# Triangular inverse of the RWKV-7 chunks: all four quadrants of the array, with the second head's chunk halves exchanged and its transpose made by a product with the identity

## The chip, the cores and the metric

The kernel runs on one core of a Trainium2 chip. The metric is the device time of one execution in microseconds (us). The engines meant below are TensorE (PE, and PEld for its weight loads), VectorE (DVE), ScalarE (ACT), GpSimd (POOL) and SyncE (SP), whose queue issues most of the DMAs.

## The reference, cut to what matters

A decoder trunk of two layers over 512 tokens of width 1024. Each layer is a SwiGLU half step, a mixing stage, and a second SwiGLU half step. The mixing stage projects the tokens once and gives the columns to three branches: attention, RWKV-7 time mixing with 4 heads of 64, and a short convolution. The change touches the RWKV-7 branch alone. Its reference is a scan over tokens:

```python
def step(S, inp):
    r_t, w_t, k_t, v_t, kk_t, a_t = inp
    s_kk = jnp.einsum('bhvk,bhk->bhv', S, kk_t)
    S = (S * w_t[:, :, None, :] - s_kk[..., None] * (kk_t * a_t)[:, :, None, :]
         + v_t[..., None] * k_t[:, :, None, :])
    return S, jnp.einsum('bhvk,bhk->bhv', S, r_t)
```

Because each step also subtracts a rank-one term that depends on the state, a chunked form needs the inverse of a unit triangular matrix for each chunk and head.

## The kernel before

The 512 tokens are 8 chunks of 64. The 4 heads are two pairs, `rwkv(0)` and `rwkv(1)`; each is a Python generator. In a pair, `e` is the head (0 or 1), `b` a block of two chunks, `c` the chunk within its block, and `rows[0]`, `rows[1]` are partitions 0 to 63 and 64 to 127. So each pair works on 16 small matrices of 64 by 64 (2 heads, 4 blocks, 2 chunks), held in tiles of 128 partitions: partitions `rows[c]` hold chunk `c`, and `e`, `b` are in the free direction.

A pair's steps, with the names that are used below:

- `pairs` makes `B_` and `K_` (line 824, PE to `ps_c`; line 828, DVE). `LT` is the triangular part of `B_`.
- `LT` goes to DRAM as `dl` (line 836, SP), and its 16 by 16 diagonal blocks come back as `G` (line 846, eight DMAs). DVE inverts the blocks by elimination: 30 short instructions on `elim` and `inv` (lines 853 and 854). The result goes out as `di` (line 856) and comes back as `C_` (line 859, eight DMAs).
- `px` (`ps_xv`, line 893) is `K_` times the centred values `vN`; `alphas` (`ps_ta`, lines 867 and 878) transposes a part of `AR`. Both are copied by ACT into the tile `AX`. `beN` and `kaN` are two more transposes.
- `T_` (line 907) is the block diagonal inverse and `TT` (line 908) its transpose, made by DVE. Two levels then widen it: `ps_x` is `LT` times `T_`, masked to `X` (line 921); at level 0 `ps_t` corrects `T_` (line 925); at both levels `ps_tt` corrects `TT` (line 928).
- `ps_w` (`ps_w2` in the code, line 935) applies `TT` to `AX`, and ACT negates it back into `AX` (line 936), which is `Wn` from there.
- `ps_gn` gives `GT` and `N` (lines 953 and 954, DVE); `ps_o` (lines 964 to 969) gives `RT` and `y` (lines 971 and 972); then `ps_s` and `St` (lines 977 and 978) carry the state from chunk to chunk, six times; `ps_ys` adds the state's part to `y`; a group norm follows (`ps_v`, `gnrs`) and the gate (`ps_g`).

Products made by the helper `each`, by line 893 and by line 935 read `rows[c]` and write `rows[c]`: two of the array's four 64 by 64 quadrants. `ps_c`, `ps_gn` and `ps_o` read and write both halves in all four combinations.

What sets the order. The big projections of the stage (`ps_mm`, from the generator `products`) are interleaved with the three branches by a credit: each `yield` of a branch states a cost, and product steps are put in between in proportion, from the totals `RWKV_WORK`, `ATT_WORK` and `FILL_WORK` at the top. A scheduler then orders each engine's instructions; within `manual_schedule` PE's rows keep the order written. `behind` adds a wait so that neighbours on the array start together. Each engine runs its queue in order. Accumulators of a pair have the tag `r0` or `r1`, two buffers each, so that a new one waits until an older one has been read.

Of the kernel before, what the change touches and what calls it, by code (L numbers as in the profile page):

```python
# [32 lines left out]
GROUPS = ((0, 12), (12, 22))  # L33
RWKV_WORK, ATT_WORK, FILL_WORK = 29.8, 15.2, 129.6

# [22 lines left out]
def trunk_kernel(ctx, tc, ins, out, layers=L, phases=("ffn1", "mix", "ffn2")):  # L58
# [21 lines left out]
    def psum(shape, name, tag="x"):  # L80
        return ps.tile(shape, F32, name=name, tag=tag, bufs=2)
# [503 lines left out]
    def mix(l, hn, ss, mp, then, ready):  # L585
# [170 lines left out]
        def rwkv(q):  # L756
# [78 lines left out]
            dl = dram.tile([P, 2 * NB, CH], F32, name="dl", tag=f"dl{q}", bufs=2)  # L835
            nc.sync.dma_start(dl, LT.rearrange("p e b t -> p (e b) t"))
            NM = CH // BASE
# [36 lines left out]

            def alphas():
                pt = tmajor(AR[:, 0].rearrange("p c t -> p (c t)"), "ps_ta")
                for e in range(2):
                    nc.scalar.copy(AX[:, e, :, 0], pt[:, :, rows[e]])

# [5 lines left out]
            vN = S(q, "vN")  # L885
            stt(vN.rearrange("p (b d) -> p b d", d=CH), mv.unsqueeze(2).to_broadcast([P, 2 * NB, CH]), -1.0 / CH, pt, ALU.mult, ALU.add)
            vN = blocks(vN)
            yield 0.4
            px = psum([P, 2, NB, CH], "ps_xv", R)
            for e in range(2):  # L890
                for b in range(NB):
                    for c in range(2):
# [14 lines left out]
            tt(T4, C_.unsqueeze(2).to_broadcast([P, 2 * NB, NM, BASE]), msk, ALU.mult)  # L907
# [3 lines left out]
            def each(name, lhs, rhs):  # L911
                pt = psum([P, 2, NB, CH], name, R)
                for e in range(2):
                    for b in range(NB):
                        for c in range(2):
                            mm(pt[rows[c], e, b], lhs[rows[c], e, b], rhs[rows[c], e, b], start=True, stop=True)
                return pt

            for lev in range(2):
                px = each("ps_x", LT, T_)  # L920
                tt(X, px, rep2(f"lev{lev}", NB), ALU.mult)
                yield 1.3
                if lev == 0:
                    p1 = each("ps_t", TT, X)
                    tt(T_, T_, p1, ALU.subtract)
                    yield 1.3
                p2 = each("ps_tt", X, TT)
                tt(TT, TT, p2, ALU.subtract)
                yield 1.3
            Wn = AX.rearrange("p e b a t -> p e b (a t)")  # L930
            for e in range(2):
                pt = psum([P, NB, P], "ps_w2", R)
                for b in range(NB):
                    for c in range(2):
                        mm(pt[rows[c], b], TT[rows[c], e, b], Wn[rows[c], e, b], start=True, stop=True)
                other = nc.scalar.mul(Wn[:, e], pt, -1.0)
                yield 1.1

# [4 lines left out]
            with tc.manual_schedule(engines={mybir.EngineType.PE}):  # L943
                for b in range(NB):
                    for c, e in ce:
                        m = mm(pgs[c][rows[e], 0, b], Wn[rows[c], e, b, :CH], beN[rows[c], b, rows[e]], start=True, stop=True)
                        behind(m, other)
                    for c, e in ce:
                        mm(pgs[c][rows[e], 1, b], kaN[rows[c], b, rows[e]], vN[rows[c], b, rows[e]], start=True, stop=False)
                    for c, e in ce:  # L950
                        mm(pgs[c][rows[e], 1, b], beN[rows[c], b, rows[e]], Wn[rows[c], e, b, CH:], start=False, stop=True)
            for c, pg in enumerate(pgs):
# [8 lines left out]
            with tc.manual_schedule(engines={mybir.EngineType.PE}):  # L961
                for b in range(NB):
                    for c, e in ce:
                        m = mm(pos[c][rows[e], 0, b], Wn[rows[c], e, b, :CH], B_[rows[c], e, b, 1], start=True, stop=True)
                        behind(m, other)
                    for c, e in ce:
                        mm(pos[c][rows[e], 1, b], Wn[rows[c], e, b, CH:], B_[rows[c], e, b, 1], start=True, stop=False)
                    for c, e in ce:
                        mm(pos[c][rows[e], 1, b], vN[rows[c], b, rows[e]], K_[rows[c], e, b, 1], start=False, stop=True)
# [402 lines left out]
```

## Time and profile before

| what | value |
|---|---|
| median of 3 runs | 1913.05 us (1911.36 to 1914.67) |
| the profiled execution | 1913.21 us, of which its span is 1911.2 us |
| PE busy | 1878.8 us, 98% of the span |
| DVE busy | 1399.8 us, 73% |
| ACT busy | 837.0 us, 44% |
| POOL busy | 130.7 us, 7% |

In the profile a line is a line of the kernel, an arrow `a<-b` means that `a` is written from `b`, a tile's number is left out, and the release of an idle engine stands in brackets. A 64 by 64 product in fp32 is two records on PE and PEld, so 16 products of a group are 32 records; a transpose of 128 by 128 is one record, and so is a product of the projections. `ps_w2` appears as `ps_w`.

### The profile page before, as it was taken

The page shows a single profiled execution, that of the slowest core. Times are in us where ns is not written, and L with a number is a line of the kernel's source. Part 1 is how long each engine was busy: PE and PEld are TensorE (multiplying, and loading weights), DVE is VectorE, ACT ScalarE, POOL GpSimd, SP SyncE. Part 2 cuts the span into 40 slices and gives each one's busy share as a digit, 9 for nine tenths or more (in the row PEclk, how much of TensorE's full clock was granted, in tenths as well). Part 3 has the DMA queues.
Part 4 walks back from the last instruction along what each step waited for, and adds up shares of the span by engine and source line. Part 5 has one row for each costly group of instructions (what it writes and reads, how often), then busy time and mean ns, then how long its engine had stood idle before and what let it go on. Part 6 is the DMA issues. An engine that isn't in the chain of part 4 may idle for free. (4 is left out here: it accounts for less than half of the span.)

```text
span 1911.2 us, 37042 instructions
## 1 busy us (share of the span) xinstructions
PE 1878.8 (98%) x15504; PEld 1741.7 (91%) x15504; DVE 1399.8 (73%) x2181; ACT 837.0 (44%) x1264; POOL 130.7 (7%) x212
## 2 busy tenths in 40 slices
PE   8999999999999999999999999999999999999999
PEld 7998899897888999899899989989878899988998
DVE  7687687758976877677877776876599667864862
ACT  4443255346322554155345514544562235532551
POOL 0101100100000001110100020010000000110000
PEclk8999999999999999999999999999999999999999
DMA  7767877521312476887727678781321315774741
GB/s 300 245 168 221 271 198 229 168 70 45 79 43 81 123 198 176 278 218 199 264 62 193 171 260 242 191 278 42 93 61 49 88 34 163 209 217 130 198 140 59
DMA packets 104326, 308.46 MB, mean 161 GB/s; under 512 B 23392, under 2 KB 24416, under 8 KB 103136
## 3 DMA queue, kind: packets, MB, share of 16 engines
q1 hardware_dynamic: 75936, 203.33, 32.9%
q0 software_dynamic: 28224, 102.77, 21.7%
q8 instruction: 121, 1.98, 0.4%
q14 instruction: 45, 0.37, 0.1%
HBM read 302.66 MB, written 3.41 MB: 160 GB/s over the span
## 5 line engine op out<-in xcount | busy, mean ns | idle before, releaser
L101 ACT CAST wH<-wraw 128x1024 fp32r<-128x1024 f32 (+2 forms) x292 | 268.4, 922 | 512.6 <-PE ps_mm L91 176.8
L102 DVE TENSOR_TENSOR wL<-wraw,wH 128x1024 fp32r<-128x1024 f32 (+2 forms) x292 | 308.1, 1058 | 96.9 <-ACT wH L101 95.8
L90 PE MATMUL ps_mm<-actH,wH 128*128 128x512 f32 (+1 forms) x784 | 288.5, 368 | 0.0
L91 PE MATMUL ps_mm<-actL,wH 128*128 128x512 f32 (+1 forms) x784 | 288.0, 367 | 0.0
L92 PE MATMUL ps_mm<-actH,wL 128*128 128x512 f32 (+1 forms) x784 | 288.0, 367 | 0.0
L441 PE MATMUL ps_d<-comH,wH 128*128 128x256 f32 x816 | 226.8, 278 | 1.6 <-ACT wH L101 0.8
L443 PE MATMUL ps_d<-comH,wL 128*128 128x256 f32 x816 | 225.8, 277 | 2.3 <-DVE wL L102 2.3
L442 PE MATMUL ps_d<-comL,wH 128*128 128x256 f32 x816 | 225.5, 276 | 0.0
L98 PE MATMUL ps_mm<-hnH,wH 128*128 128x256 f32 x1040 | 214.0, 286 | 5.1 <-ACT hnH L101 2.9
L98 PE MATMUL ps_mm<-hnL,wH 128*128 128x256 f32 x1040 | 211.8, 283 | 0.0
L98 PE MATMUL ps_mm<-hnH,wL 128*128 128x256 f32 x1040 | 209.5, 281 | 0.5 <-DVE wL L102 0.5
L163 DVE SCALAR_TENSOR_TENSOR wada<-wada,crep 128x1024 f32<-128x1024 f32 x140 | 168.0, 1220 | 47.8 <-DMA wada<-in_wadaT 47.6
L102 DVE TENSOR_TENSOR wL<-sum,wH 128x1024 fp32r<-128x1024 f32 x102 | 124.8, 1224 | 74.9 <-ACT wH L101 74.7
L98 PEld LDWEIGHTS ps_mm<-hnH,wH 128*128 128x128 f32 x1040 | 159.5, 190 | 16.1 <-issue 8.2
L92 PEld LDWEIGHTS ps_mm<-actH,wL 128*128 128x128 f32 x784 | 147.8, 189 | 24.4
L90 PEld LDWEIGHTS ps_mm<-actH,wH 128*128 128x128 f32 x784 | 147.8, 189 | 24.2
L91 PEld LDWEIGHTS ps_mm<-actL,wH 128*128 128x128 f32 x784 | 147.8, 189 | 24.1
L101 ACT CAST wH<-sum 128x1024 fp32r<-128x1024 f32 x102 | 107.5, 1054 | 140.3 <-PE ps_d L442 60.1
L98 PEld LDWEIGHTS ps_mm<-hnL,wH 128*128 128x128 f32 x1040 | 160.2, 190 | 6.7 <-issue 5.7
L98 PEld LDWEIGHTS ps_mm<-hnH,wL 128*128 128x128 f32 x1040 | 160.1, 190 | 4.1 <-issue 2.9
L441 PEld LDWEIGHTS ps_d<-comH,wH 128*128 128x128 f32 x816 | 153.2, 188 | 3.9 <-ACT wH L101 1.4
L443 PEld LDWEIGHTS ps_d<-comH,wL 128*128 128x128 f32 x816 | 153.2, 188 | 2.9 <-DVE wL L102 2.9
(402 smaller groups left out, 4237.3 us busy)
## 6 DMA issues: line engine op xcount, KB each, us to landing
wada<-in_wadaT POOLq DMA_DIRECT2D x128, 512.0 KB, 4.9
wraw<-in_wmi SPq DMA_DIRECT2D x40, 512.0 KB
wraw<-in_w2p SPq DMA_DIRECT2D x36, 512.0 KB
wraw<-in_w1p SPq DMA_DIRECT2D x32, 512.0 KB
wraw<-in_w1o SPq DMA_DIRECT2D x32, 384.0 KB
wraw<-in_w2o SPq DMA_DIRECT2D x32, 384.0 KB
wraw<-in_w1i SPq DMA_DIRECT2D x20, 512.0 KB
wraw<-in_w1o SPq DMA_DIRECT2D x32, 320.0 KB
```

Source lines behind the costliest of these rows:

```text
L90: mm(acc, wH, xH, start=start, stop=False)
L91: mm(acc, wH, xL, start=False, stop=False)
L92: mm(acc, wL, xH, start=False, stop=stop)
L98: mm(acc[:, sl], w[a][:, k], x[b][:, sl], start=start and n == 0 and sl is HALVES[0], stop=stop and n == 2, skip_group_check=True)
L101: nc.scalar.copy(hi, src)
L102: nc.vector.tensor_sub(lo, src, hi.bitcast(F32))
L163: stt(w, w, 1.0, crep, ALU.mult, ALU.mult, accum_out=out_)
L441: mm(pt[:, i], wH, x[k][0], start=start and i + k == 0, stop=False, skip_group_check=True)
L442: mm(pt[:, i], wH, x[k][1], start=False, stop=False, skip_group_check=True)
L443: last = mm(pt[:, i], wL, x[k][0], start=False, stop=k == 3, skip_group_check=True)
```

## The change

All products of the inverse go through a new helper `quads`, which takes two accumulators and lets the caller name, for each of the 16 products, the output half, the accumulator, and the operands. It writes the rows out in the order block, head, chunk. For head 1 the halves of the chunks are exchanged in `T_`, `TT`, `X` and `AX`: chunk `c` of head `e` lies in partitions `rows[c ^ e]`. So four neighbours on the array use four different quadrants. Each product now leaves two accumulators, one for each half of the array's rows, and DVE or ACT reads them in two pieces of 128x256 instead of one of 128x512.

What follows from the exchange:

- `dl` is stored by three DMAs instead of one, with head 1's and head 0's parts of the lower half exchanged.
- `alphas` is gone: `ps_ta` is 16 products with a 64 by 64 identity instead of four transposes of 128 by 128, and ACT copies it in four pieces instead of two.
- `TT` is no longer made by DVE's transpose: `flip` multiplies `T_` by the identity (`ps_T`) and ACT copies the two accumulators. At level 0 a second `flip` takes the place of the product `ps_tt` and of DVE's subtraction. At level 1 `ps_tt` stays as it was, on two quadrants.
- `ps_gn` and `ps_o` read `Wn` at its exchanged place.
- The yields and `RWKV_WORK` (29.8 to 30.5) are adapted.

```diff
-RWKV_WORK, ATT_WORK, FILL_WORK = 29.8, 15.2, 129.6
+RWKV_WORK, ATT_WORK, FILL_WORK = 30.5, 15.2, 129.6
...
-            nc.sync.dma_start(dl, LT.rearrange("p e b t -> p (e b) t"))
+            nc.sync.dma_start(dl[rows[0]], LT[rows[0]].rearrange("p e b t -> p (e b) t"))
+            for e in range(2):
+                nc.sync.dma_start(dl[rows[1], (1 - e) * NB : (2 - e) * NB], LT[rows[1], e])
...
-            def alphas():
-                pt = tmajor(AR[:, 0].rearrange("p c t -> p (c t)"), "ps_ta")
-                for e in range(2):
-                    nc.scalar.copy(AX[:, e, :, 0], pt[:, :, rows[e]])
+            def quads(name, one, other, w=CH):
+                pts = [psum([P, NB, w], name, R) for _ in range(2)]
+                with tc.manual_schedule(engines={mybir.EngineType.PE}):
+                    for b in range(NB):
+                        for e in range(2):
+                            for c in range(2):
+                                out_, k, lhs, rhs = one(e, b, c)
+                                behind(mm(pts[k][rows[out_], b], lhs, rhs, start=True, stop=True), other)
+                return pts
+
+            def ident(k):
+                return cst("ident")[rows[k], rows[k]]
...
-                        mm(px[rows[c], e, b], K_[rows[c], e, b, 0], vN[rows[c], b, rows[e]], start=True, stop=True)
-            nc.scalar.copy(AX[:, :, :, 1], px)
+            for k, px in enumerate(quads("ps_xv", lambda e, b, c: (c ^ e, c, K_[rows[c], e, b, 0], vN[rows[c], b, rows[e]]), centred)):
+                nc.scalar.copy(AX[:, k, :, 1], px)
             yield 1.3
-            alphas()
+            for e, pt in enumerate(quads("ps_ta", lambda e, b, c: (c ^ e, e, AR[rows[e], 0, 2 * b + c], ident(e)), None)):
+                for r in range(2):
+                    nc.scalar.copy(AX[rows[r], r ^ e, :, 0], pt[rows[r]])
...
-            nc.vector.transpose(TT.rearrange("p e b t -> p (e b t)"), T_.rearrange("p e b t -> p (e b t)"))
+
+            def flip(other):
+                for k, pt in enumerate(quads("ps_T", lambda e, b, c: (c ^ e, c, T_[rows[c], c ^ e, b], ident(c)), other)):
+                    last = nc.scalar.copy(TT[:, k], pt)
+                return last
+
+            flip(None)
+            yield 1.0
...
-                px = each("ps_x", LT, T_)
-                tt(X, px, rep2(f"lev{lev}", NB), ALU.mult)
+                for k, px in enumerate(quads("ps_x", lambda e, b, c: (c ^ e, c, LT[rows[c], e, b], T_[rows[c], c ^ e, b]), None)):
+                    made = tt(X[:, k], px, rep(f"lev{lev}", NB), ALU.mult)
                 yield 1.3
                 if lev == 0:
-                    p1 = each("ps_t", TT, X)
-                    tt(T_, T_, p1, ALU.subtract)
+                    for k, p1 in enumerate(quads("ps_t", lambda e, b, c: (c, c ^ e, TT[rows[c ^ e], c, b], X[rows[c ^ e], c, b]), made)):
+                        made = tt(T_[:, k], T_[:, k], p1, ALU.subtract)
                     yield 1.3
-                p2 = each("ps_tt", X, TT)
-                tt(TT, TT, p2, ALU.subtract)
-                yield 1.3
+                    flip(made)
+                    yield 1.0
+                else:
...
+                                    mm(p2[r, k, b], X[r, k, b], TT[r, k, b], start=True, stop=True)
+                    made = tt(TT, TT, p2, ALU.subtract)
+                    yield 1.3
...
-                        mm(pt[rows[c], b], TT[rows[c], e, b], Wn[rows[c], e, b], start=True, stop=True)
-                other = nc.scalar.mul(Wn[:, e], pt, -1.0)
-                yield 1.1
+            pts = quads("ps_w2", lambda e, b, c: (c, c ^ e, TT[rows[c ^ e], c, b], Wn[rows[c ^ e], c, b]), made, P)
+            for k, pt in enumerate(pts):
+                other = nc.scalar.mul(Wn[:, k], pt, -1.0)
+            yield 2.2
```

The order moves in the mixing stage of both layers alike; the rows here are of layer 0.

First, DVE's queue where the first pair's `GT` and `N` meet the second pair's elimination (`elim` and `inv`). Before:

```order
L854 TENSOR_TENSOR inv<-inv,elim 64x4x12
L953 TENSOR_TENSOR GT_5415<-ps_gn,con 128x4x64
L954 TENSOR_TENSOR N_5416<-ps_gn,pc_5090 128x4x64
L953 TENSOR_TENSOR GT_5415<-ps_gn,con 128x4x64
L954 TENSOR_TENSOR N_5416<-ps_gn,pc_5090 128x4x64
L957 COPY St_5520<-N_5416 128x64
L853 TENSOR_TENSOR elim<-G,inv 64x39
L854 TENSOR_TENSOR inv<-inv,elim 64x3x13
L853 TENSOR_TENSOR elim<-G,inv 64x28
L854 TENSOR_TENSOR inv<-inv,elim 64x2x14
L853 TENSOR_TENSOR elim<-G,inv 64x15
L854 TENSOR_TENSOR inv<-inv,elim 64x15
```

The same place with the change:

```order
L856 TENSOR_TENSOR inv<-inv,elim 64x4x12
L855 TENSOR_TENSOR elim<-G,inv 64x39
L856 TENSOR_TENSOR inv<-inv,elim 64x3x13
L855 TENSOR_TENSOR elim<-G,inv 64x28
L856 TENSOR_TENSOR inv<-inv,elim 64x2x14
L855 TENSOR_TENSOR elim<-G,inv 64x15
L856 TENSOR_TENSOR inv<-inv,elim 64x15
L965 TENSOR_TENSOR GT_5488<-ps_gn,con 128x4x64
L966 TENSOR_TENSOR N_5489<-ps_gn,pc_5090 128x4x64
L965 TENSOR_TENSOR GT_5488<-ps_gn,con 128x4x64
L966 TENSOR_TENSOR N_5489<-ps_gn,pc_5090 128x4x64
```

The last six instructions of the second pair's elimination stood behind the first pair's `GT` and `N`, and now all thirty stand ahead of them.

Second, DVE's queue a little later, in the first pair's scan (`St`), where the second pair's `T_` is made from `C`. Before:

```order
L978 SCALAR_TENSOR_TENSOR St_5520<-ps_s,pc_5090,N_5416 128x64 x4
L102 TENSOR_TENSOR wL<-wraw,wH 128x768
L978 SCALAR_TENSOR_TENSOR St_5520<-ps_s,pc_5090,N_5416 128x64 x2
L907 TENSOR_TENSOR T_6229<-C,con 128x512
L984 TENSOR_TENSOR y_5523<-y_5523,ps_ys 128x448
```

With the change:

```order
L990 SCALAR_TENSOR_TENSOR St_5593<-ps_s,pc_5090,N_5489 128x64 x3
L915 TENSOR_TENSOR T_6321<-C,con 128x512
L990 SCALAR_TENSOR_TENSOR St_5593<-ps_s,pc_5090,N_5489 128x64
L102 TENSOR_TENSOR wL<-wraw,wH 128x768
L990 SCALAR_TENSOR_TENSOR St_5593<-ps_s,pc_5090,N_5489 128x64 x2
L996 TENSOR_TENSOR y_5596<-y_5596,ps_ys 128x448
```

The second pair's `T_` stood behind all six steps of the first pair's scan, and now it stands behind the third.

Third, PE's queue at the same place. Before, from the last step of the scan:

```order
L977 MATMUL ps_s<-St_5520,GT_5415 64x64 x2
L983 MATMUL ps_ys<-RT_5522,St_5520 64x64 x14
L98 MATMUL ps_mm<-hnL,wH 128x256 x2
L98 MATMUL ps_mm<-hnH,wL 128x256 x2
L98 MATMUL ps_mm<-hnH,wH 128x256
L916 MATMUL ps_x<-T_6229,B_5945 64x64 x16
```

With the change, from the fifth step:

```order
L884 MATMUL ps_T<-con,T_6321 64x64 x4
L989 MATMUL ps_s<-St_5593,GT_5488 64x64 x2
L884 MATMUL ps_T<-con,T_6321 64x64 x12
L98 MATMUL ps_mm<-hnH,wL 128x256
L989 MATMUL ps_s<-St_5593,GT_5488 64x64 x2
L995 MATMUL ps_ys<-RT_5595,St_5593 64x64 x14
L884 MATMUL ps_x<-T_6321,B_6012 64x64 x16
```

The second pair's `flip` now stands ahead of the fifth and sixth steps of the scan, and fewer projection products (`ps_mm`) stand around it.

More of the change, by code (lines that the diff above doesn't have):

```diff
@@ L885, in rwkv @@
             vN = S(q, "vN")
-            stt(vN.rearrange("p (b d) -> p b d", d=CH), mv.unsqueeze(2).to_broadcast([P, 2 * NB, CH]), -1.0 / CH, pt, ALU.mult, ALU.add)
+            centred = stt(vN.rearrange("p (b d) -> p b d", d=CH), mv.unsqueeze(2).to_broadcast([P, 2 * NB, CH]), -1.0 / CH, pt, ALU.mult, ALU.add)
             vN = blocks(vN)
             yield 0.4
[L889 to L892, printed above, removed]
-                        mm(px[rows[c], e, b], K_[rows[c], e, b, 0], vN[rows[c], b, rows[e]], start=True, stop=True)
-            nc.scalar.copy(AX[:, :, :, 1], px)
+            for k, px in enumerate(quads("ps_xv", lambda e, b, c: (c ^ e, c, K_[rows[c], e, b, 0], vN[rows[c], b, rows[e]]), centred)):
+                nc.scalar.copy(AX[:, k, :, 1], px)
             yield 1.3
-            alphas()
+            for e, pt in enumerate(quads("ps_ta", lambda e, b, c: (c ^ e, e, AR[rows[e], 0, 2 * b + c], ident(e)), None)):
+                for r in range(2):
+                    nc.scalar.copy(AX[rows[r], r ^ e, :, 0], pt[rows[r]])
             yield 0.4
@@ L926, in rwkv @@
                     yield 1.3
-                p2 = each("ps_tt", X, TT)
-                tt(TT, TT, p2, ALU.subtract)
-                yield 1.3
-            Wn = AX.rearrange("p e b a t -> p e b (a t)")
[L931 to L936, printed above, removed]
-                yield 1.1
+                    flip(made)
@@ new lines, in rwkv @@
+                    yield 1.0
+                else:
+                    p2 = psum([P, 2, NB, CH], "ps_tt", R)
+                    with tc.manual_schedule(engines={mybir.EngineType.PE}):
+                        for k in range(2):
+                            for b in range(NB):
+                                for r in rows:
+                                    mm(p2[r, k, b], X[r, k, b], TT[r, k, b], start=True, stop=True)
+                    made = tt(TT, TT, p2, ALU.subtract)
+                    yield 1.3
@@ L945, in rwkv @@
                     for c, e in ce:
-                        m = mm(pgs[c][rows[e], 0, b], Wn[rows[c], e, b, :CH], beN[rows[c], b, rows[e]], start=True, stop=True)
+                        m = mm(pgs[c][rows[e], 0, b], Wn[rows[c], c ^ e, b, :CH], beN[rows[c], b, rows[e]], start=True, stop=True)
                         behind(m, other)
@@ L950, in rwkv @@
                     for c, e in ce:
-                        mm(pgs[c][rows[e], 1, b], beN[rows[c], b, rows[e]], Wn[rows[c], e, b, CH:], start=False, stop=True)
+                        mm(pgs[c][rows[e], 1, b], beN[rows[c], b, rows[e]], Wn[rows[c], c ^ e, b, CH:], start=False, stop=True)
             for c, pg in enumerate(pgs):
```

11 lines of the change are left out of this document (2 added, 9 removed).

## The prediction

> **What bounds the kernel now.** I read the page first, then the stretches of the first layer's mixing stage and the chain of waits of PE, then the timeline there. Columns of a stretch: its length, then busy time and count of each engine, TensorE's granted clock, DMA.
>
> ```profile
> PE 1878.8 (98%) x15504; PEld 1741.7 (91%) x15504; DVE 1399.8 (73%) x2181; ACT 837.0 (44%) x1264; POOL 130.7 (7%) x212
> 500.00:510.00 10.00, 10.00 (x78) 8.70 (x75) 10.00 (x25) 5.27 (x8) 0.00 (x0) 1.00 0.01 2
> 550.00:560.00 10.00, 10.00 (x140) 8.37 (x139) 8.48 (x10) 2.57 (x4) 0.00 (x0) 1.00 0.03 11
> PE ps_bo L611 <- DVE bonus L800: 1.8, 4, 0.6
> ```
>
> PE is the bound of the whole, but not of each stage. Around 500 us DVE is full (10.00 of 10), and PE waits for it at `ps_bo`, once for each of the four pairs. Around 555 us, where the second pair's inverse runs, PE is full and DVE isn't. So PE time saved in the second pair should count; saved in the first pair it counts only if nothing else in that pair's chain is late.
>
> **What the array saves.** Rows: start, length, engine, line, records.
>
> ```profile
> 528.76 1.01 PEld L916 LDWEIGHTS ps_x<-T,B 64*64 64x64 f32 x32
> 532.93 1.78 PEld L935 LDWEIGHTS ps_w<-AX,TT 64*64 64x64 f32 x32
> 535.76 0.21 PEld L946 LDWEIGHTS ps_gn<-beN,AX 64*64 64x64 f32 x8 [0.17 <-ACT AX L936]
> 537.04 0.21 PEld L951 LDWEIGHTS ps_gn<-AX,beN 64*64 64x64 f32 x8
> 522.90 0.64 PEld L824 LDWEIGHTS ps_c<-AR,iP 64*64 64x64 f32 x22 [0.67 <-DVE B L828]
> 529.84 0.42 PEld L867 LDWEIGHTS ps_vN<-con,v 128*128 128x128 f32 x4
> 557.64 0.40 PE L98 MATMUL ps_mm<-hnL,wH 128*128 128x256 f32 x2
> 559.95 0.39 PE L98 MATMUL ps_mm<-hnH,wL 128*128 128x256 f32 x2
> ```
>
> On two quadrants a product of 32 records takes 1.01 us, and `ps_w`, twice as wide, 1.78. On four, `ps_gn`: the first and the last of its 12 rows of 8 records start 1.28 apart, so 0.116 a row and 0.46 for 32. `ps_c`, as wide as `ps_w`, has 22 records in 0.64, so 32 in 0.93. The new products read and write halves in the same four combinations with an accumulator for each half, as `ps_gn` does, so I take its rate. Per pair: `ps_xv`, two `ps_x`, `ps_t`, and the flip that replaces `ps_tt` at level 0 save 5 x 0.55 = 2.75; `ps_w` saves 0.85; the added flip costs 0.46; `ps_ta` costs 0.46 for four transposes of 0.42 in all. That is **3.1 us a pair, 12.4 in four pairs**. A `ps_mm` takes (559.95 - 557.64) / 20 = 0.115.
>
> **The second pair** has `ps_mm` between all its products, 15 to 24 of them, so copies and DVE's pieces stay covered and its saving counts: `ps_x` twice, `ps_t`, the exchange for `ps_tt`, `ps_w`, less one flip, 4 x 0.55 + 0.85 - 0.46 = 2.6 us a layer. Its `ps_xv` runs inside the first pair's stretch.
>
> **The first pair.** Here there is little between the products, so I follow the chain. DVE's rows before:
>
> ```profile
> 523.43 0.68 DVE L907 TENSOR_TENSOR T<-C,con 128x512 f32<-128x512 f32 x1
> 526.09 0.68 DVE L921 TENSOR_TENSOR X<-ps_x,con 128x512 f32<-128x512 f32 x1
> 526.69 1.27 DVE L828 TENSOR_TENSOR K<-ps_c,con 128x512 f32<-128x512 f32 x2
> 528.02 0.69 DVE L925 TENSOR_TENSOR T<-T,ps_t 128x512 f32<-128x512 f32 x1
> 532.10 0.69 DVE L928 TENSOR_TENSOR TT<-TT,ps_tt 128x512 f32<-128x512 f32 x1
> 532.70 0.16 DVE L853 TENSOR_TENSOR elim<-G,inv 64x15 f32<-64x15 f32 x1
> 538.29 0.41 DVE L953 TENSOR_TENSOR GT<-ps_gn,con 128x256 f32<-128x256 f32 x1
> 539.62 0.18 DVE L957 COPY St<-N 128x64 f32<-128x64 f32 x1
> 540.79 0.17 DVE L854 TENSOR_TENSOR inv<-inv,elim 64x15 f32<-64x15 f32 x1
> 539.74 0.21 PEld L964 LDWEIGHTS ps_o<-B,AX 64*64 64x64 f32 x8 [0.85 <-DVE N L954]
> 534.13 0.60 ACT L936 ACTIVATE AX<-ps_w 128x512 f32<-128x512 f32 x1 [12.13 <-PE ps_w L935]
> L878 ACT COPY AX<-ps_ta x8: 365/372/378, 494.9 to 1474.4; 128x256 f32<-128x256 f32 x8
> ```
>
> With the change: `T_` is there at 524.1 as before. The flip takes 0.46; `ps_x` needs the two accumulators that the flip filled, so it waits for two ACT copies of 0.37: it ends at 525.9. `X` in two pieces (0.41 each, spaced 0.33 as `GT` and `N` are) ends at 526.8, where it ended at 526.8 before. `ps_t` follows; DVE has half of `K` (0.6) and the equally wide reduction `mv` ahead of the subtraction, which ends at 528.7, as before. Then flip, two copies, `ps_x`, `X`: 531.4. `ps_tt`, still 1.0 us on two quadrants, starts behind the first half of `X` at 531.05; `TT` ends at 532.8, as before. What the array gains here goes to the copies, and DVE, which loses a transpose and a subtraction (0.69) and gains some 0.4 in pieces, waits instead.
>
> So the second pair's elimination begins at 532.7 as before, but now all thirty instructions stand ahead of `GT`. They took 5.6 us (to 538.29) and 1.3 (539.62 to 540.96): `GT` starts at 539.6 and `ps_o`, 1.45 behind it as before, at **541.05 instead of 539.74**. PE has until then `ps_w` (to 533.8), a wait for ACT's two negations (0.60 each, to 535.0), `ps_gn` to 536.5, eight transposes, six `ps_mm`: done at 538.25. It waits 2.8 us.
>
> ```profile
> 541.02 0.46 SPq L856 DMA_DIRECT2D di<-inv  x1
> 543.93 3.62 SPq L859 DMA_DIRECT2D C<-di  x8
> 546.07 0.95 DVE L102 TENSOR_TENSOR wL<-wraw,wH 128x768 fp32r<-128x768 f32 x1
> 549.11 0.69 DVE L907 TENSOR_TENSOR T<-C,con 128x512 f32<-128x512 f32 x1 [0.65 <-DMA C<-di]
> 543.07 0.28 DVE L978 SCALAR_TENSOR_TENSOR St<-ps_s,pc,N 128x64 f32<-128x64 f32 x1 [0.91 <-PE ps_s L977]
> 544.00 0.28 DVE L978 SCALAR_TENSOR_TENSOR St<-ps_s,pc,N 128x64 f32<-128x64 f32 x1 [0.65 <-PE ps_s L977]
> 549.86 1.15 PE L916 MATMUL ps_x<-T,B 64*64 64x64 f32 x32
> 551.19 1.12 PE L611 MATMUL ps_v<-gnsq,con 128*128 128x512 f32 x2
> 572.28 0.65 PE L935 MATMUL ps_w<-AX,TT 64*64 64x128 f32 x6
> ```
>
> `di` leaves when the elimination ends, 541.0 before and 539.65 now, and `T_` came 8.1 us behind it: 547.75. The scan runs at 0.93 a step from 543.3, so DVE reaches `T_` (behind the third `St`) at 545.7 and stands there; the fourth `St`, the flip and the fifth `ps_s` are queued behind it. PE runs dry at 546.7 and waits 1.7. A weight's `wL` (0.95) stands before the fifth `St`; the scan, `ps_ys` and `ps_x` end at 551.4 (before 550.9), with 13 fewer `ps_mm` done since `ps_o`, 6 of which had been done ahead of it. `ps_v` starts some 1.4 behind `ps_ys`, at 552.4 instead of 551.19. From there PE is full. Its work to the point where `ps_w` ends and equally many `ps_mm` are done (572.9 before) is `ps_v` and `ps_g` 1.9, `ps_t`, flip, `ps_x` 1.4, `ps_tt` 1.0, `ps_w` 0.93, 111 `ps_mm` 12.8 and some 1.5 of entering and leaving quadrants: 571.9. **Net: 1.0 us a layer**, so the first pair's new waits eat 1.6 of the second pair's 2.6.
>
> **Hidden edits.** The added ACT copies (two flips of two, `ps_ta` in four pieces for two, `ps_xv` in two for one: 2.4 us a pair) lie in ACT's idle time, 12.13 us ahead of its first negation; without it they would add 2.4 to the chain.
>
> ```profile
> 522.88 0.55 SPq L836 DMA_DIRECT2D dl<-B  x1
> 526.27 3.61 SPq L846 DMA_DIRECT2D G<-dl  x8
> 525.26 0.91 DVE L102 TENSOR_TENSOR wL<-wraw,wH 128x768 fp32r<-128x768 f32 x1
> ```
>
> Of three `dl` stores one goes when the first half of `B` is made, and the last is issued by 524.0, not 523.4: `G` starts 0.6 later at most. Its last piece lands about 1.6 behind the last issue (as `C`, from 547.55 to 549.11), near 532.1; elimination needs it at 532.7. A fill weight's load now stands ahead of `G` on SP; the `wL` that frees its buffer ends at 526.2, and earlier without the transpose, about when `G` can start. Without this cover, up to 1 us a layer. `RWKV_WORK` and the yields only spread the same `ps_mm` otherwise. What PE saves before 520 us (`ps_xv` of the first pair) goes into the waits at `ps_bo`: nothing, at most 0.55 a layer.
>
> **Layer 1** has the same order. One thing differs:
>
> ```profile
> 589.11 0.33 PE L977 MATMUL ps_s<-St,GT 64*64 64x64 f32 x4 [1.36 <-ACT y L972]
> 1526.45 0.33 PE L977 MATMUL ps_s<-St,GT 64*64 64x64 f32 x4 [2.17 <-ACT y L972]
> 1527.24 0.63 PE L98 MATMUL ps_mm<-y0L,wH 128*128 128x256 f32 x2
> 1520.00:1530.00 10.00, 7.83 (x57) 7.23 (x57) 3.87 (x7) 2.48 (x4) 0.00 (x0) 0.84 0.49 138
> ```
>
> After a wait of 2.17 us the granted clock drops and 16 `ps_mm` take about twice as long: some 1.6 us lost. In layer 0 the wait of 1.36 costs no clock. The change puts 6 more `ps_mm` (0.7 us) ahead of this `ps_s`, and 6 fewer behind, so the wait would be 1.5. I count half of 1.6.
>
> **Sum.** Against the profiled execution (1913.21, close to the median 1913.05; the span is 1911.2): 2 x 1.0 + 0.8 = 2.8, so **1910.4 us**.
>
> **Rivals.** *Full saving:* DVE or the elimination is earlier than I think, PE has no new waits, and 12.4 us go: 1900.8; with half of it, 1906. For it: PE at 98%, and DVE has less to do. Against it: the elimination behind `TT` is a chain of 6.9 us that nothing shortens. *The clock, slower:* the new waits at `ps_o` (2.8) and at the flip (1.7) in both layers halve the clock as at 1526. Price 1.6 each, 6.4 in four places, less the 2.0 gained and without the 0.8: 1917.6. It decides from a wait between 1.36 and 2.17. For it: 2.8 is above that; against it: a slow stretch behind `ps_o` only fills the wait for `T_`. [...] *Not four at once:* if identity products and exchanged halves run at 1.01 us, the flips add 1.0 a pair and the first pair's chain grows by 2.7 a layer: about 1919. `ps_gn` speaks against it.
>
> **Chances.** Forecast 0.55, over 1906 to 1915 from the unknown ends (`G` late 2 us in two layers, `ps_xv` counted 1.1, the clock 0.8 either way, and 1 us a layer for my chain); full or half saving 0.22; clock 0.17; not four at once 0.06. A measurement here can tell 0.2%, 3.8 us, from no change: faster is below 1909.2, slower above 1916.9. Faster: 0.22 and a quarter of the forecast, 0.36; slower: half the clock and the last, 0.15; same 0.49. The range leaves out the lower part of the full saving and the upper end of the last two: 1902 to 1917.
>
> **What would show it.** `ps_gn`'s rate (32 records in about 0.46) in `ps_x`, `ps_t`, `ps_T`; elimination starting near 532.7 and `GT` behind all of it; PE waiting over 2 us at `ps_o` for `N` and over 1 us at `ps_T` for `T_`; none between the second pair's products. I am wrong if `GT` starts before 538.3, if `ps_T` finds `T_` ready, or if the clock drops at `ps_o`.

## The result, and the profile after

| | before | changed |
|---|---|---|
| median | 1912.80 us (7 executions, 1911.36 to 1914.67) | 1921.27 us (7 executions, 1917.65 to 1923.62) |
| ratio to before | | 1.0041, 95% interval 1.0029 to 1.0052 |
| profiled execution: time, span | 1913.21, 1911.2 | 1921.27, 1919.3 |
| mean granted clock in the profile | 0.996 | 0.992 |
| from `ps_bo` to `ps_g` of the second pair, layer 0, layer 1 | 89.15, 91.04 | 92.07, 95.51 |

The change makes the kernel **slower by about 8 us**; 1910.4 was forecast, with a range of 1902 to 1917. The last row runs from the second pair's `ps_bo`, with which its work on the chunks begins, to its gate `ps_g`: by it the mixing stages of the two layers hold 2.9 and 4.5 us. The rest, 0.7 us, lies outside these stretches, where the profiles differ by more than that without a known cause (from the end of the one to the start of the other stretch 847.3 us before, 849.3 with the change, and 845.5 to 848.4 in the kernels below).

The page's first part for the changed kernel, then the chain of waits of PE (waited for, us in total, times, longest):

```profile
PE 1876.9 (98%) x15744; PEld 1737.6 (91%) x15744; DVE 1395.9 (73%) x2185; ACT 847.0 (44%) x1292; POOL 130.7 (7%) x212
PE ps_o L976 <- DVE St L969: 5.1, 2, 2.6
PE ps_s L989 <- ACT y L984: 2.2, 2, 1.8
PE ps_s L989 <- DVE St L990: 2.2, 2, 1.1
```

The page hardly differs: PE is busy 98% in both, and busy for 1.9 us less. What is new is a wait at `ps_o`, 5.1 us in two places (before: 1.2), and a second wait at `ps_s`, 1.1 us in each layer. PE's timeline of the changed kernel in layer 0 shows what follows the first:

```profile
536.08 0.29 PE L958 MATMUL ps_gn<-beN,AX 64*64 64x64 f32 x8
536.20 0.30 PE L961 MATMUL ps_gn<-vN,kaN 64*64 64x64 f32 x8
541.24 0.34 PE L976 MATMUL ps_o<-B,AX 64*64 64x64 f32 x8 [2.55 <-DVE St L969]
541.64 0.51 PE L976 MATMUL ps_o<-B,AX 64*64 64x64 f32 x8
541.86 0.50 PE L979 MATMUL ps_o<-B,AX 64*64 64x64 f32 x8
552.76 1.13 PE L611 MATMUL ps_v<-gnsq,con 128*128 128x512 f32 x2 [0.51 <-ACT gnsq L1000]
```

`ps_gn`'s rows of 8 records start 0.12 apart, `ps_o`'s equal rows 0.22 apart: soon after the wait PE runs at about half speed. The granted clock by stretches says for how long. Columns as before: length, busy time of PE, PEld, DVE, ACT, POOL, granted clock, DMA. The stretches are cut at the places where the clock changes:

```profile
538.14:541.55 3.41, 0.86 (x26) 0.69 (x28) 2.81 (x13) 0.52 (x2) 0.00 (x0) 1.00 0.08 19
541.55:544.97 3.42, 3.42 (x96) 3.30 (x88) 0.76 (x2) 0.64 (x2) 0.00 (x0) 0.50 0.10 12
589.34:592.75 3.41, 2.07 (x18) 1.76 (x19) 2.20 (x5) 1.24 (x3) 0.00 (x0) 1.00 0.44 124
592.75:596.17 3.42, 3.42 (x19) 3.08 (x18) 1.48 (x3) 1.05 (x1) 0.00 (x0) 0.50 0.40 145
1531.42:1534.84 3.42, 1.25 (x11) 0.97 (x10) 2.91 (x5) 1.44 (x3) 0.00 (x0) 1.00 0.38 111
1534.84:1538.25 3.41, 2.68 (x14) 2.60 (x15) 0.87 (x3) 0.00 (x0) 0.00 (x0) 0.50 0.52 156
1538.25:1541.66 3.41, 3.41 (x19) 3.07 (x18) 2.07 (x3) 1.04 (x1) 0.00 (x0) 0.50 0.02 6
```

The clock is halved in whole pieces of 3.41 us, five of them in the mixing stages (the fifth at 1483.63, behind layer 1's `ps_o`); before there is one, at 1526.82. By the granted clock of 0.50 a piece at half clock is up to 1.7 us of TensorE time lost (half of 3.41), an estimate; four more pieces are up to 6.8 us.

The second pair's wait in layer 1, in the timeline of the changed kernel:

```profile
1530.13 1.05 ACT L101 CAST wH<-wraw 128x1024 fp32r<-128x1024 f32 x1 [5.58 <-DMA wraw<-in_wmo]
1531.21 1.22 DVE L102 TENSOR_TENSOR wL<-wraw,wH 128x1024 fp32r<-128x1024 f32 x1 [4.61 <-ACT wH L101]
1532.35 0.75 DVE L983 TENSOR_TENSOR RT<-ps_o,AR 128x256 f32<-128x256 f32 x2
1532.80 0.70 ACT L984 COPY y<-ps_o 128x256 f32<-128x256 f32 x2 [1.63 <-DVE RT L983]
1533.22 0.33 PE L989 MATMUL ps_s<-St,GT 64*64 64x64 f32 x4 [1.78 <-ACT y L984]
1535.57 0.48 PE L989 MATMUL ps_s<-St,GT 64*64 64x64 f32 x4 [1.11 <-DVE St L990]
```

Read upwards from the first `ps_s`: it waits for `y`, `y` for `RT`, and `RT` is queued on DVE behind a `wL` whose weight comes by DMA (`wraw`). TensorE's saving did not make that weight come earlier where the two profiles can be compared: in layer 0 the same cast of `wraw` starts at 586.01 before and at 586.47 with the change. The second `ps_s`, 1.11 us, waits for a `St` that is queued on DVE behind the next weight's `wL`, 0.96 us long.

### The profile page after: what moved, and what is told of

It is laid out like the page before. It is cut to its first block, busy times and chain, and to the rows that moved or that the text cites. A ratio compares the mean times of both kernels' runs of the same rounds, so it can differ in the third digit from the quotient of the medians.

```text
span 1919.3 us, 37594 instructions
## 1 busy us (share of the span) xinstructions
PE 1876.9 (98%) x15744; PEld 1737.6 (91%) x15744; DVE 1395.9 (73%) x2185; ACT 847.0 (44%) x1292; POOL 130.7 (7%) x212
## 3 DMA queue, kind: packets, MB, share of 16 engines
HBM read 302.66 MB, written 3.41 MB: 159 GB/s over the span
```

## The experiments

"Ratio" is to the kernel before, timed beside each kernel on the same chip. The two stage columns are `ps_bo` to the second pair's `ps_g` in the profile, with the number of pieces at half clock inside; kernels with the new first pair do six more `ps_mm` (0.7 us) in there, 389 for 383.

| kernel | median us | ratio, 95% interval | layer 0 | layer 1 |
|---|---|---|---|---|
| before | 1912.80 | | 89.15, 0 | 91.04, 1 |
| changed | 1921.27 | 1.0041 (1.0029 to 1.0052) | 92.07, 2 | 95.51, 3 |
| e5 changed again | 1919.26 | 1.0026 (1.0016 to 1.0037) | 91.40, 1 | 94.60, 3 |
| e1 order | 1910.40 | 0.9989 (0.9980 to 0.9998) | 88.70, 0 | 90.19, 1 |
| e2 fill | 1913.53 | 1.0005 (0.9996 to 1.0014) | 88.92, 1 | 89.46, 1 |
| e6 order and fill | 1908.34 | 0.9975 (0.9963 to 0.9986) | 87.25, 0 | 87.25, 0 |
| e3 second pair only | 1907.12 | 0.9975 (0.9965 to 0.9985) | 88.07, 0 | 87.63, 0 |
| e4 first pair only | 1914.29 | 1.0011 (1.0003 to 1.0020) | 92.13, 1 | 90.53, 0 |
| e7 second pair only, fill | **1904.92** | 0.9954 (0.9941 to 0.9966) | 87.21, 0 | 87.01, 0 |
| e8 before, fill | 1909.72 | 0.9983 (0.9974 to 0.9992) | 87.32, 0 | 88.65, 0 |
| e9 flip apart | 1916.58 | 1.0015 (1.0006 to 1.0025) | 89.12, 0 | 89.98, 0 |
| e10 flip, order, fill | 1907.72 | 0.9971 (0.9960 to 0.9983) | 88.57, 0 | 89.24, 0 |
| e11 before, late `GT` | 1914.09 | 1.0011 (1.0001 to 1.0021) | 89.35, 0 | 92.02, 1 |

The profiles of e2 (1909.72) and e9 (1909.72) are of the fastest of their executions, so their stage columns are shorter than the median would give; those of e3 (1909.87) and e8 (1911.15) are of the slowest.

**e1, the order.** `el` are the second pair's thirty elimination instructions, `marks` the first pair's first `GT`, first `St`, and the two `RT`; `behind(a, b)` puts `a` behind `b`. The lines that collect them are left out:

```diff
...
+            if q:
+                behind(got["marks"][0], el[23])
+                for m in el[24:]:
+                    behind(m, got["marks"][1])
+                behind(got["marks"][2], el[-1])
```

> The changed kernel, with VectorE's order at one place as it was before: in each layer the last six of the second pair's thirty elimination instructions stand behind the first pair's GT, N and first St, and ahead of RT. Theory A (the clock): the new wait of 2.55 us at ps_o halves TensorE's clock, in both layers. Here the wait is 2.55 - 1.3 = 1.25 us, less than the 1.36 that cost no clock at 589 us before; the windows 540 to 550 and 1480 to 1490 (0.83 now) go back to 1.00, and the first pair's stretch from ps_bo to ps_v loses the 1.3 of the wait and most of the 1.7 of the clock: 2 to 3 us a layer, 1915 to 1917. Theory B (the pieces): the copies and half-size pieces make the first pair's chain longer, and the slow clock only fills the wait for T_; then at most the order itself comes back, 0 to 1 us a layer, 1919 to 1921.

1910.40: faster than either theory gave, and 10.9 below the changed kernel. PE's rows in its timeline:

```profile
540.71 0.34 PE L983 MATMUL ps_o<-B,AX 64*64 64x64 f32 x8 [1.45 <-DVE St L976]
540.84 0.33 PE L986 MATMUL ps_o<-B,AX 64*64 64x64 f32 x8
```

The wait is 1.45 us, the rows behind it stay 0.13 apart, and no piece is halved at `ps_o` in either layer. Undoing the place of six instructions of about 0.2 us gives back the whole loss; theory B's time is out. The gain is not all at `ps_o`, though: the scheduler then also puts the second pair's `T_` behind the scan again and 17 more `ps_mm` ahead of `ps_v` (97 from `ps_bo`, for 80), and layer 1's first wait at `ps_s` is 0.44 instead of 1.78. So this run does not test whether the slow clock behind `ps_o` only filled the wait for `T_`. The mean clock over the executions goes from 0.9923 to 0.9963, which is 7.7 us of TensorE time.

**e2, the fill.** Only two of the second pair's yields are moved, so that more `ps_mm` (the fill) stand ahead of its first two `ps_s`:

```diff
-            yield 2.2
+            yield 2.8 if q else 2.2
...
-                yield 0.6
+                yield 0.5 if q else 0.6
```

> The changed kernel with two of the second pair's yields moved: 2.8 for 2.2 behind ps_o and 0.5 for 0.6 in the scan, so that 48 instead of 42 ps_mm stand ahead of its first ps_s and 12 instead of 6 ahead of the second; nothing is added. Theory A: the waits at these two ps_s (0.45 and 1.11 us in layer 0, 1.78 and 1.11 in layer 1) set off the halved clock at 590 to 600 and 1530 to 1550 (1.7 and 3.4 us of clock lost); with the fill in front the waits are under 0.6 in layer 0, and the clock stays in at least one of the layers: 1917 to 1919.5. Theory B: the clock's drop there costs nothing that counts, 1920.5 to 1922.

1913.53: a larger gain than theory A gave (1917 to 1919.5). The first pair still waits 2.56 and 2.50 us at `ps_o`, and a piece is halved behind it in both layers; in the second pair neither a wait over 0.3 us nor a halved piece is left. So the second pair, too, lost 3.1 and 5.5 us (from the first pair's `ps_v` to the second's `ps_g` 55.35 and 57.66 in the changed kernel, 52.30 and 52.19 here, with 309 `ps_mm` in all four).

**e3 and e4, one pair each.** The new code under `if q in NEW:`, the old under `else:`; `RWKV_WORK` is 30.15, between the two.

> The first pair by the old code (two quadrants, DVE's transpose), the second pair by the new code. Theory A: the first pair's stretch ends as before, without a drop of the clock at 540 and 1480, and the second pair's saving of 2.6 us a layer counts, less up to 1.7 where the clock falls at its ps_s: 1907 to 1911, faster than both kernels. Theory B: the second pair's own pieces eat its saving, 1912 to 1915.

> The first pair by the new code, the second by the old. Theory A: the first pair's stretch is longer by what the changed kernel shows from ps_bo to ps_v, 2.6 and 3.6 us, with the clock at 0.83 behind ps_o in both layers, and the second pair stands as before: 1917 to 1920. If the loss lies in the second pair, 1913 to 1915.

The second pair alone: 5.8 us faster than before, at the fast end of theory A's range. The first pair alone: 1.4 slower, less than expected; its two waits of 2.16 and 2.17 us at `ps_o` halve nothing in the profile. The two effects add up to -4.4, the two changes together give +8.5: **most of the loss is in neither part alone, but comes with both together.** The clock says the same: over their executions the two kernels have the mean clock of the kernel before (0.9963 and 0.9962, before 0.9963), and the changed kernel has 0.9923. Here is how the 2.16 that halves nothing lies; the stretches of e4 on the grid of its halved piece:

```profile
540.04:543.45 3.41, 1.85 (x98) 1.81 (x99) 1.71 (x7) 0.00 (x0) 0.00 (x0) 1.00 0.12 26
543.45:546.87 3.42, 3.39 (x31) 2.72 (x30) 1.89 (x5) 2.46 (x5) 0.00 (x0) 1.00 0.11 10
587.83:591.24 3.41, 1.63 (x16) 1.37 (x15) 2.55 (x4) 1.78 (x4) 0.00 (x0) 1.00 0.36 110
591.24:594.65 3.41, 3.41 (x19) 3.07 (x18) 1.44 (x3) 0.26 (x1) 0.00 (x0) 0.50 0.59 169
```

`ps_o` starts at 541.6, so only 1.56 of the 2.16 lie in the piece from 540.04; PE is busy for 1.85 us of it, and the next piece runs at full clock (in e1 a piece with 1.85, at 1523.55, was followed by a halved one). At 587.83 it is busy for 1.63, and the next piece is halved, though the wait there is shorter (1.78).

**e5, the changed kernel again.**

> The changed kernel once more, unedited. Theory A2 (the grid): TensorE's clock is halved for whole pieces of 3.41 us on a grid that is fixed within an execution and lies differently in each; a piece is halved when TensorE was busy for less than about 0.6 of the piece before it. Then the places with a halved clock need not be those of the first profile (541.6, 592.8, 1483.6, 1534.8 to 1541.7 us): the waits of 2.55 us at ps_o halve nearly always, those at ps_s in some executions only, every halved piece begins a whole number of 3.41 us behind the others, and the times of single executions go with their mean clock (0.001 of it is 1.9 us). Rival (the wait alone decides): the same four places again, the clock 0.992 in every execution. Median 1919 to 1922 by both.

1919.26, and the grid lies otherwise: pieces are halved at 543.67, 1482.34, 1533.54 and 1536.95, and none in layer 0's second pair, whose waits are the same as in the first profile (0.36 and 1.12, there 0.45 and 1.11). From its stretches and its timeline:

```profile
591.46:594.87 3.41, 2.19 (x20) 1.89 (x21) 2.08 (x4) 1.12 (x3) 0.00 (x0) 1.00 0.60 136
594.87:598.29 3.42, 3.42 (x32) 3.03 (x31) 2.41 (x4) 1.05 (x1) 0.00 (x0) 1.00 0.35 133
554.83 0.70 PE L611 MATMUL ps_v<-gnsq,con 128*128 128x512 f32 x1 [0.51 <-ACT gnsq L1000]
608.57 0.59 PE L1012 MATMUL ps_g<-gd,gw 128*128 128x512 f32 x1
```

The same work from the first pair's `ps_v` to the second's `ps_g`, 309 `ps_mm` in both, takes 53.74 us here, and 55.35 in the first profile:

```profile
608.11 0.59 PE L1012 MATMUL ps_g<-gd,gw 128*128 128x512 f32 x1
```

So one halved piece costs 1.61 us in one and the same kernel, where PE has work to fill it. "The wait alone decides" is out: nearly equal waits halve here and not there, and in e4 1.78 us did and 2.16 did not. The times follow the clock, if loosely: e5's eight executions go from 1922.23 us at a mean clock of 0.992 to 1916.17 and 1918.33 at 0.995. Up to `ps_v`, with one halved piece behind `ps_o` in both, layer 0 takes 0.9 us more in e5 than in the first profile; there the second pair's `T_` came later, 9.3 us behind the elimination instead of 8.2.

**e6, e7, e8: both fixes, and a control.** The edits of e1 and e2 together; e3 with e2's yields; the kernel before with the same fill (yields 2.9 and 0.5).

> The changed kernel with both edits of before: the last six elimination instructions behind the first pair's GT and N, and the second pair's fill moved ahead of its first two ps_s (yields 2.8 and 0.5). If the two losses are apart, this is the time with the order alone (1910.4) less the second pair's waits there (0.43 and 1.12 us, down to about 0.5) and the clock that falls at them in about one layer of two (1.7): 1907 to 1908.5. If the one only hides what the other loses, no change to 1910.4.

> The new code for the second pair alone, with the second pair's fill moved ahead of its first two ps_s (yields 2.8 and 0.5). With the new code for the second pair alone the waits there were 0.39 and 0.89 us in layer 0 and 0.90 in layer 1, without a drop of the clock in the profile; most of them go: 0.6 to 1 us a layer, 1905 to 1906. If other engines end last there anyway, 1907.

> The kernel before with the second pair's fill alone moved (yields 2.9 and 0.5, the same numbers of ps_mm between its products as in the two kernels with the moved fill): a control that says how much of their gain has nothing to do with the quadrants. Its waits there were 1.36 and 0.44 us in layer 0 and 2.17 in layer 1, the last with the halved clock: 1.2 us of waits a layer and about 1.7 of clock in one layer go, 1909 to 1910.5. Rival: it gains less than 1 us, 1912 to 1913, since before the change these waits were not what ends last.

All three as the first theory of each had it: 1908.34, 1904.92 (0.08 below its range), 1909.72, and no piece is halved in their mixing stages. The control shows that 2.8 of the 7.6 us by which e7 beats before have nothing to do with the quadrants: the wait at `ps_s` was there before the change. These 2.8 are waits and not the clock: e8's mean clock is that of before (0.9961), and in the two stages PE is idle for 4.6 us, where it was 7.3. The other 4.8, 2.4 a layer, are what the new second pair is worth at most, since the mean clocks of e7 and e8 (0.9968 and 0.9961) leave 1.3 of them to the clock. TensorE's own part can be read in the two stages, first of e8, then of e7:

```profile
519.49:606.81 87.32, 85.65 (x1375) 76.08 (x1376) 61.01 (x121) 22.98 (x37) 0.00 (x0) 1.00 0.27 76
1453.83:1542.48 88.65, 85.71 (x1376) 76.12 (x1377) 60.98 (x121) 22.99 (x37) 0.00 (x0) 1.00 0.26 75
516.18:603.39 87.21, 84.08 (x1435) 73.95 (x1436) 59.84 (x122) 25.19 (x44) 0.00 (x0) 1.00 0.27 76
1449.53:1536.54 87.01, 84.02 (x1435) 73.91 (x1436) 59.98 (x122) 25.08 (x44) 0.00 (x0) 1.00 0.26 76
```

PE is busy for 1.57 and 1.69 us less a layer, with the same 383 `ps_mm`. And e7 beats e6, so with both fixes the new first pair still costs 3.4 us.

**e9 and e10, the copies.** The exchange products take accumulators of another tag, so that `ps_x` need not wait until ACT has read them. e9 is the changed kernel with this alone, e10 has the edits of e1 and e2 as well:

```diff
-            def quads(name, one, other, w=CH):
-                pts = [psum([P, NB, w], name, R) for _ in range(2)]
+            def quads(name, one, other, w=CH, tag=R):
+                pts = [psum([P, NB, w], name, tag) for _ in range(2)]
...
-                for k, pt in enumerate(quads("ps_T", lambda e, b, c: (c ^ e, c, T_[rows[c], c ^ e, b], ident(c)), other)):
+                for k, pt in enumerate(quads("ps_T", lambda e, b, c: (c ^ e, c, T_[rows[c], c ^ e, b], ident(c)), other, tag="x")):
```

> The changed kernel with the exchange products (ps_T) of both pairs in the accumulators that attention used, so that ps_x no longer waits for ACT's two copies; the scheduler then also puts all but the last elimination instruction ahead of GT as before the edit, and T_ behind the scan. Theory (the copies are on the first pair's chain): from B to TT the first pair's chain gets 2 x 0.6 to 0.8 us shorter (10.6 and more now: ps_x starts 1.2 behind ps_T in the first profile), GT and ps_o come 1.2 to 1.6 earlier, and the wait at ps_o, with 4 more ps_mm ahead of it, is 1 to 1.6 us instead of 2.55: the clock stays. From ps_bo to ps_v 2 to 3 us less a layer, and the second pair as in the changed kernel (waits, and sometimes the clock): 1911 to 1915. If the copies are not on the chain, 1918 to 1921.

> The changed kernel with three edits: the exchange products in the accumulators that attention used, the last six elimination instructions behind the first pair's GT and N, and the second pair's fill moved ahead of its first two ps_s. Theory (the first pair's chain is longer by the copies, which is why the new code for the second pair alone is 3.4 us faster than the new code for both with the same two other edits): the copies leave the chain, 0.6 to 1.6 us a layer, 1905 to 1907.5. If the new code of the first pair loses elsewhere, 1908.3 as without this edit.

The first pair's chain on DVE, in the changed kernel's timeline (`B` is the second pair's and stands on DVE just ahead of the first pair's `T_`; it serves as the starting mark):

```profile
520.59 1.27 DVE L828 TENSOR_TENSOR B<-ps_c,con 128x512 f32<-128x512 f32 x2
527.28 0.74 DVE L932 TENSOR_TENSOR T<-T,ps_t 128x256 f32<-128x256 f32 x2
530.48 0.76 DVE L928 TENSOR_TENSOR X<-ps_x,con 128x256 f32<-128x256 f32 x2 [1.85 <-PE ps_x L884]
532.22 0.69 DVE L943 TENSOR_TENSOR TT<-TT,ps_tt 128x512 f32<-128x512 f32 x1 [0.99 <-PE ps_tt L942]
539.68 0.41 DVE L965 TENSOR_TENSOR GT<-ps_gn,con 128x256 f32<-128x256 f32 x1
```

and in e10's:

```profile
520.38 1.27 DVE L828 TENSOR_TENSOR B<-ps_c,con 128x512 f32<-128x512 f32 x2
526.16 0.73 DVE L938 TENSOR_TENSOR T<-T,ps_t 128x256 f32<-128x256 f32 x2
528.32 0.76 DVE L934 TENSOR_TENSOR X<-ps_x,con 128x256 f32<-128x256 f32 x2
530.14 0.69 DVE L949 TENSOR_TENSOR TT<-TT,ps_tt 128x512 f32<-128x512 f32 x1 [1.07 <-PE ps_tt L948]
```

From `B` to `TT` 11.63 us become 9.76: the copies are on the chain, as the theory said, for 1.9 us a layer. The time hardly follows. e10 misses its range by 0.2 and is 0.6 below e6, which their spread does not tell from nothing; its two stages are even 1.3 and 2.0 us longer than e6's. 15 fewer `ps_mm` then stand in the shorter stretch up to `ps_v`, and the waits come back elsewhere (1.33 and 0.44 us at the second pair's `ps_s` in layer 0). e9 misses its range: 1916.58, with a mean clock of 0.9949 over its executions. Its waits at `ps_o` are 2.18 and 1.48 us and the second one at `ps_s` stays (1.12), so it probably still loses pieces in many executions, though none in the one profiled, whose mean clock is 0.996. What else the new first pair costs (e10 against e7: 2.8 us) stays open: PE is idle for 6.3 and 6.7 us in e10's stages and for 3.1 and 3.0 in e7's, and which step of the new code opens these waits was not separated.

**e11, the order in the kernel before.** `got["early"]` holds the first pair's two `GT`; they go behind the last elimination instruction, and their `N` follow:

```diff
...
+            if q:
+                for g in got["early"]:
+                    behind(g, last)
```

> The kernel before, with VectorE's order at one place as the change made it: all thirty elimination instructions of the second pair ahead of the first pair's GT and N, and T_ between its St. The scheduler then puts 8 more ps_mm ahead of ps_o. Theory (the order costs only by the wait that it opens, and that by the clock): ps_o comes 1.3 us later, 0.9 of it is filled, the wait is 0.6 + 1.3 - 0.9 = 1.0 us, the clock stays at 1.00 there, and the time is that of before within 2 us: 1912 to 1915. Rival (the late GT costs its 1.3 us a layer, or more, whatever fills the wait): 1915.5 to 1918.

1914.09, as the theory said, and 2.5 above the 1911.61 of the kernel before on the same chip (by the interval 0.2 to 4). `ps_o` waits 0.91, and the clock stays there. So the order costs about 1 us a layer where fill covers it, and not the 5 that undoing it gave back in e1.

## Why the prediction was wrong, step by step

- **The array's rate: right; the second pair's saving: too large.** The weight loads of a `ps_x`, 32 records, take 0.56 us on four quadrants, and on two 1.01. The product between `ps_mm`, before and changed:

```profile
560.27 1.15 PE L916 MATMUL ps_x<-T,B 64*64 64x64 f32 x32
561.35 0.38 PE L98 MATMUL ps_mm<-hnH,wH 128*128 128x256 f32 x1
```

```profile
563.00 0.69 PE L884 MATMUL ps_x<-T,B 64*64 64x64 f32 x32
563.62 0.38 PE L98 MATMUL ps_mm<-hnH,wH 128*128 128x256 f32 x1
```

  From its start to that of the next `ps_mm` 1.08 and 0.62: 0.46 a product, where 0.55 was counted, and 0.62 for the added flip, where 0.46 was. With these the forecast's own sum gives 4 x 0.46 + 0.85 - 0.62 = 2.1 us a layer instead of 2.6. e7 against e8, where the second pair's `ps_xv` counts too, showed at most 2.4 in the time, and 1.6 and 1.7 in PE's busy time.
- **The first pair's chain ends at the same time: wrong by 1.1 us.** Two of DVE's rows before:

```profile
521.57 1.28 DVE L828 TENSOR_TENSOR B<-ps_c,con 128x512 f32<-128x512 f32 x2
529.96 0.69 DVE L921 TENSOR_TENSOR X<-ps_x,con 128x512 f32<-128x512 f32 x1 [0.32 <-PE ps_x L916]
```

  From `B` to `TT` it took 10.53 before and 11.63 after. Forecast was that the array's gain goes to the copies. At the second exchange it took more: from `T` to `X` 3.20 instead of 1.94, and `ps_tt` gave only 0.4 back. e10 showed the place.
- **Elimination, `GT`, `ps_o`: the order and the wait right, the times by luck.** 539.6 and 541.05 with a wait of 2.8 were forecast; it is 539.68, 541.24 and 2.55. `ps_v` was forecast at 552.4 and came at 552.76. Two errors hide each other here: the chain is 1.1 longer, and the second pair's `ps_bo` came 1.0 earlier than before, 0.7 of it because six `ps_mm` that stood ahead of it now stand behind it. In e5, where `ps_bo` came 0.1 later than before, the wait is the same and the times are 540.82 and 542.37:

```profile
540.82 0.41 DVE L965 TENSOR_TENSOR GT<-ps_gn,con 128x256 f32<-128x256 f32 x1
542.37 0.34 PE L976 MATMUL ps_o<-B,AX 64*64 64x64 f32 x8 [2.55 <-DVE St L969]
```

- **From `ps_v` on: badly added.** By differences, a `ps_v` 1.2 later, 13 more `ps_mm` (1.5) and 2.6 saved give +0.1 us at `ps_gn`. The forecast built the stretch up from parts instead and set the sum against a measured end, which gave 1.0 earlier. The 1.5 of entering and leaving quadrants in that sum was the author's estimate and is shown by no run as such; the changed kernel's `ps_x` above gives 0.25 (it starts at 563.00, 0.09 us behind the place of a next `ps_mm`, and takes 0.62 for the forecast's 0.46), so about 1.25 for the five products in the sum. Measured is 0.7 later (576.59 against 575.89, the same number of `ps_mm` done): `ps_v` 1.57 later, 11 more `ps_mm` (1.27), and 2.1 saved.
- **The clock behind the second pair's waits: the step that failed.** The forecast counted nothing for it in layer 0, and in layer 1 half of 1.6 as a gain of 0.8; the runs showed one or two halved pieces in layer 0 and three in layer 1. Its words against the rival were that "a slow stretch behind `ps_o` only fills the wait for `T_`". For the pieces behind `ps_o` that nearly holds: in layer 0 of the first profile the wait of 1.7 at the flip is gone, and from `ps_o` to `ps_v` it took 11.52 where 11.35 was forecast. In layer 1 and in both layers of e5 it took 12.1 to 12.6, but there `T_` came 8.9 to 9.4 us behind the elimination instead of the 8.1 that were forecast, and PE still waited for it at the flip, 0.33 to 0.91. The second pair is where it fails: there PE was to be full from `ps_v` on, and a piece costs 1.61 (e5). For it the forecast took the wait of 1.36 that halves nothing and the 2.17 that does as two sides of a threshold, and expected the wait at `ps_s` to shrink. It shrank, to 0.45 and 1.78, but a second one of 1.11 opened behind it, where the forecast itself had put six fewer `ps_mm` and counted no wait, and in layer 0 of the first profile the two in one piece were enough. e2, which takes away these waits and pieces and leaves those at `ps_o`, gave back 7.7 us (5.7 against e5), where the forecast was off by 10.9; the same edit was worth 2.8 before the change (e8), so some 3 to 5 of the 10.9 came with it here. The outcome is near the rival *The clock, slower*, which was given 0.17: its price of 1.6 a piece was right (1.61 in e5), but three of the five places were others than it named, and these are the ones that cost time.

The clock is a large part of the loss, and not all of it. Over its executions the changed kernel's mean clock is 0.9923 (e5: 0.9938), and that of the kernel before in the executions beside the experiments 0.9963 (0.9961). By the difference times the span this is 7.7 and 4.4 us of TensorE time, where the changed kernel was 8.5 and 6.7 us slower; but the part of it that only fills the wait for `T_` costs no time, and how much that is in each execution is not shown. The waits themselves are no less: in the profiled stages PE is idle for 15.9 us, before for 7.3. Of these the forecast had counted 2.8 and 1.7 a layer, and of the clock nothing. One slip in a rival: half of 12.4 saved is 1907.0, not 1906.

## What to carry to other kernels

Before moving work on a TensorE that is 98% busy, list the places where it will wait for 1 to 3 us. Here each could cost up to 1.6 us more than it lasted, where nothing else ended the stretch. Filling the second pair's places with work that is there anyway was worth 2.8 us in the old kernel and 2.1 to 7.7 in the others, where the new second pair itself was worth at most 4.8. By these runs a gain on TensorE counts only where nothing but TensorE ends the stretch: only the second pair's gain came through, and the version that changes only that pair, with its fill moved, is the fastest.

## What the hardware showed that was not expected

In these profiles the clock changes on a grid of 3.41 us that is fixed within an execution: in the changed kernel the halved pieces begin at 541.55, 592.75, 1483.63 and 1534.84, the last three 51.20, 942.08 and 993.29 us behind the first, which is 15, 276 and 291 times 3.4133. Of the pieces at full clock in the mixing stages of all the profiles here, the eleven with up to 1.64 us of PE's busy time were all followed by a half-clock piece, and none of those with 2.10 or more. Of the ten between, two were (1.85 and 2.07), and one with 1.66 was not. So the border lies between 1.64 and 2.10 us of the 3.41, and in there PE's busy time in the profile does not decide alone; what does is not shown. The 0.6 of a piece in e5's theory, 2.05 us, was the author's estimate: eight pieces with 1.66 to 2.03 were followed by full clock. In the kernel before:

```profile
588.16:591.57 3.41, 2.03 (x20) 1.80 (x20) 2.63 (x6) 1.44 (x3) 0.00 (x0) 1.00 0.39 115
591.57:594.99 3.42, 3.42 (x33) 3.02 (x32) 1.88 (x4) 1.05 (x1) 0.00 (x0) 1.00 0.51 153
1523.41:1526.82 3.41, 1.24 (x13) 0.98 (x12) 2.39 (x4) 1.79 (x4) 0.00 (x0) 1.00 0.14 21
1526.82:1530.24 3.42, 3.42 (x17) 3.08 (x18) 1.52 (x4) 0.64 (x1) 0.00 (x0) 0.50 0.55 145
```

Where the grid lies differs from one execution to the next (in e5, the same kernel, the piece behind layer 0's `ps_o` begins at 543.67, 2.12 us later than in the first profile, and the next ones 275, 290 and 291 pieces behind it), so nearly equal waits cost 1.6 us in one and nothing in another. Whether this makes the spread of 6 us among the changed kernel's executions is not shown: the kernel before spreads over 8 us in the twenty executions beside e5 (1909.92 to 1918.03).
